# Shift and scale of the first channel mixer: from sums on VectorE to products on TensorE

## The chip, the cores and the metric

The kernel runs on one core of one Trainium2 chip. The metric is device time in microseconds for the whole trunk: two layers at 256 tokens and 2048 channels, everything in 32-bit floats. Three runs of the kernel before gave a median of 2667.47 us (2666.54 to 2671.47).

## The reference, cut to what matters

Each layer turns a conditioning vector `c` into six vectors of 2048 values: a shift, a scale and a gate for the token mixer, and the same three for the channel mixer.

```python
c_act = jax.nn.silu(c)
for i in range(DEPTH):
    mod = c_act @ ada_w[i] + ada_b[i]
    sh_m, sc_m, g_m, sh_f, sc_f, g_f = jnp.split(mod, 6, axis=-1)
    h = modulate(rms_norm(x, norm_mix_g[i]), sh_m, sc_m)
    out = ...                     # layer 0: RWKV-7 time mix, layer 1: conformer convolution
    x = x + g_m[:, None, :] * out
    h = modulate(rms_norm(x, norm_ffn_g[i]), sh_f, sc_f)
    x = x + g_f[:, None, :] * conv_glu_ffn(h, ffn_w_up[i], ffn_w_dw[i], ffn_b_dw[i], ffn_w_down[i])
return rms_norm(x, final_norm_g)
```

`ada_w[i]` is 2048 x 12288, so one of the six pieces is a 2048 x 2048 matrix (16 MB) that meets a single vector. The change is about pieces 3 (`sh_f`) and 4 (`sc_f`) of layer 0.

## The kernel before, in words

Channels lie on the 128 partitions and tokens along the free dimension, so each of the 2048 channels belongs to one of `KT` = 16 tiles of 128 x 256. A dense weight tile is loaded as 128 x 2048 (1 MB) into a buffer named `raw`, of which there are four. It is split into a rounded part `hi` (ScalarE, line 231) and a rest `lo` (VectorE or GpSimd, line 232), and three TensorE products (lines 237 to 239) stand for one exact one.

Layer 0 runs through these stages; the times are those of the profiled execution.

- 0 to 190 us: normalise x, mix tokens, part of the k products. Here `ada_s` makes shift and scale of the token mixer as products (line 367): the vector silu(c) stands as a stationary operand of 128 x 32 (`cc`, one real column), 256 columns of `ada_w` stream past it, and four such products write to the four 32-partition groups of a PSUM tile. ScalarE copies the result out (line 371) and a product with a column of constants (line 373) adds up the four groups and turns the row of 128 values into a column.
- 190 to 412 us: the rest of k, then r and most of v, and the inverse of small triangular matrices.
- 412 to 731 us: the scan, and beside it the rest of v, group norm, gate, and half of the output projection for five tiles.
- from 731 us on: output projection, channel mixer of layer 0 (ConvGLU), layer 1.

The other pieces of the modulation are made by `ada(l, piece, f)` as jobs on VectorE: load 1 MB of the transposed weights into a `raw` buffer, multiply by silu(c) spread over all partitions and sum up in a custom instruction (line 208); for layer 0 in two halves of 1024, each followed by a short read of the accumulator. Jobs stand in the list `jobs`, and `bg(n)` takes the next n. Before the scan, the list starts with pieces 4 and 3 of all 16 tiles (32 jobs); `bg` takes ten of them in the k and r stages. For the scan, five gates (piece 2) are put in front and seven at the end, so that 34 jobs are made during it.

The order of TensorE in the scan is written by hand: each piece of work is a Python generator that yields the planned time until its next step, a heap calls the generators by planned time, and TensorE executes the products in just that order. `PD` = 13 planned units pass from one tile of the scan to the next. The orders of the other engines and of the DMA queue (all of these loads go through SyncE) are left to the tile framework's scheduler, which tracks buffers and inserts the waits. Every queue is executed in its order: an instruction that waits holds up all that stand behind it.

In the scan, `prep_gen` prepares a tile (lines 687, 688, 702, 721, 730, 736), `chain_gen` carries the state through its four chunks (lines 750, 758, 763, 769, 776), `v_gen` and `wo_gen` are dense products, and `gn_gen` is group norm and gate (lines 786, 799, 804). Masked copies out of PSUM (line 156) and the state update (lines 159 and 774) are on VectorE, other copies (lines 689, 694, 755, 765) on ScalarE.

Of the kernel before, what the change touches and what calls it, by code (L numbers as in the profile page):

```python
# [11 lines left out]
F32 = mybir.dt.float32  # L12
F32R = mybir.dt.float32r
AF = mybir.ActivationFunctionType
ALU = mybir.AluOpType
# [3 lines left out]
P = 128  # L19
T = 256  # L20
C = 2048
KT = C // P
# [27 lines left out]
BGT = 10.0  # L50
# [12 lines left out]
BGN = 16  # L63
BGT2 = 7
WACT = 1
TQ = 2
NWO = 5
# [4 lines left out]
NG = 12  # L72
# [8 lines left out]
SLAG = 2  # L81
BX = 2
CME = {mybir.EngineType.PE}
KAPPA = math.exp(-0.5)
# [27 lines left out]
def trunk_kernel(ctx: ExitStack, tc: tile.TileContext, a, out):  # L112
    nc = tc.nc
    cp = ctx.enter_context(tc.tile_pool(name="cp", bufs=1))
# [11 lines left out]
    def slot(dt=F32):  # L126
        if dt == F32R:
            return pool.tile([P, 2, SLOT], F32R, tag="s2", bufs=NS, name=nm("s"))
        return pool.tile([P, 2, SLOT], F32, tag="s2", bufs=NS, name=nm("s"))

    def slot512():
        return slot().rearrange("p a t -> p (a t)")[:, :2 * T]
# [4 lines left out]
    def raw_tile():  # L137
        return pool.tile([P, 2048], F32, tag="raw", bufs=4, name=nm("raw"))
# [24 lines left out]

    # ---- constants, parameters
    cst = cp.tile([P, NCC], F32, name="cst")
# [19 lines left out]
    geff = [cp.tile([P, 2 * KT], F32, name=f"geff{i}") for i in range(2)]  # L185
# [31 lines left out]
    jobs = []  # L217
# [4 lines left out]

    # ---- linear layers
    def split_w(r, k0, k1, step=1024, eng=None):
# [39 lines left out]
    class k_outer:  # L264
        """some outputs together, the operands fed one at a time; the weights split ahead, two operands' at once"""

# [39 lines left out]

    # ---- rms norm
    def sq_acc(st, x):
        s = t1()
        act(s, x, AF.Square)  # L310
        if st[0] is None:
            st[0] = s
        else:
            vadd(st[0], st[0], s)
# [9 lines left out]

    # ================= layer 0: time mix =================
    hs = [slot() for _ in range(KT // 2)]
# [10 lines left out]
    rstd = rstd_of(st)  # L337
# [10 lines left out]
    tg = cp.tile([P, 2, T], F32, name="tg")  # L348
    cc = slot512().rearrange("p (k m) -> p k m", k=KT)
    nc.gpsimd.memset(cc, 0.0)  # L350
# [4 lines left out]
    ahead = {}  # L355

    def ada_s(f):
        lw = slot().rearrange("p a t -> p (a t)")[:, :448]
        nc.sync.dma_start(out=lw, in_=a["lw1"][f])
        # scale and shift of tile f  # L360
        pa = ps("y")
        for q in range(2):
            r = raw_tile()
            nc.sync.dma_start(out=r, in_=a["ada_s"][f, q])
            for k in range(8):
                g, kk = k % 4, 8 * q + k
                nc.tensor.matmul(pa[32 * g:32 * g + 32, :T], lhsT=cc[:, kk, :], rhs=r[:, k * T:(k + 1) * T],  # L367
                                 start=kk < 4, stop=kk >= 12, skip_group_check=True)
        rk = load_w(a["w_k"][f])
        sb = t1()  # L370
        nc.scalar.copy(sb, pa[:, :T])
        for j in range(2):
            nc.tensor.matmul(pa[:, 256 + j:257 + j], lhsT=sb[:, j * P:(j + 1) * P], rhs=K("e4"), start=True, stop=True, skip_group_check=True)
        for j in range(2):
            piece = 1 - j
            vadd(mod(0, piece, f), pa[:, 256 + j:257 + j], pc("ada_b", piece * KT + f))
        stt(geff[0][:, f:f + 1], mod(0, 1, f), 1.0, pc("gam_mix", f), ALU.add, ALU.mult)
        ahead[f] = (lw, rk)

    ada_s(0)  # L380
    for f in range(KT):
# [11 lines left out]
        for k0 in range(0, KM, KM // 2):  # L393
            hi, lo = split_w(rk, k0, k0 + KM // 2)
            for m in range(k0, k0 + KM // 2):
                c = slice((m - k0) * P, (m - k0 + 1) * P)
                d = kps[m // 2][:, (m % 2) * T:(m % 2) * T + T]
# [25 lines left out]

    for f in range(KT):
        jobs += [(0, 4, f), (0, 3, f)]

# [9 lines left out]

    # ---- k, decay, a; A, B, K of the scan; N
    for f in range(KM, KT):
# [126 lines left out]

    # ---- inverse of the 32-blocks, all heads and chunks on partitions
    X = raw_tile()
# [65 lines left out]

    # ---- v, scan, group norm, bonus, gate
    def small(tag, w, bufs):
# [36 lines left out]
    def prep_gen(f):  # L672
        ari, bk, tt, tn = ld.pop(f)
        v = vt.pop(f)
# [5 lines left out]
        yield 0  # L680
        # products of A, R with B, K, and B, K by tokens
        for c in range(NC_):
# [12 lines left out]
            yield PU  # L695
        # off-diagonal block of the inverse
        py = ps("g")
# [5 lines left out]
        for h in range(2):  # L703
            r1 = slice(h * L + 32, h * L + 64)
            nc.scalar.copy(ysb[r1].rearrange("p c t -> p (c t)"), py[r1, :P])
        # bonus
        rk = t1()
# [6 lines left out]
        yield PU  # L714
        # centred V by tokens, in the other half of the partitions
        pvt = ps("g")
# [107 lines left out]

    # half of the output projection and residual, while the scan goes on
    def wo_gen(m):
# [10 lines left out]
    def bg_gen(n):  # L837
        for i in range(n):
            bg(1)
            yield BGT if i < BGN else BGT2  # L840

    heap, seq = [], [0]

    def at(t, g):
        heapq.heappush(heap, (t, seq[0], g))
        seq[0] += 1
# [7 lines left out]
    for fs in ((0, 1, 2, 3), (4, 5, 6, 7), (8, 9, 10, 11), (12, 13), (14, 15)):  # L854
        at((fs[-1] + 3) * PD + 3.0, gn_gen(fs))
    jobs[:0] = [(0, 2, f) for f in range(NWO)]
    jobs += [(0, 2, f) for f in range(NWO, NG)]
    at(0, bg_gen(99))
    for m in range(NWO):
        at(WO0 * PD + m * WOP, wo_gen(m))  # L860
    with tc.manual_schedule(engines={mybir.EngineType.PE}):
        while heap:
            t, _, g = heapq.heappop(heap)
            if isinstance(g, tuple):
                g = chain_gen(g[1], PD / 6)
            d = next(g, None)
            if d is not None:
                at(t + d, g)
    # ---- output projection and residual
    # gain * x, with the shift in the last columns: the products of the two are rstd-free  # L870
    def operand(l, which, f):
# [29 lines left out]

    # ---- ConvGLU
    def ffn(l, st, ops, nops):
# [54 lines left out]

    # ================= layer 1: conformer convolution =================
    ops = nops  # L960
    rstd = rstd_of(st)
# [22 lines left out]

    # n of the taps on the tensor engine, m on GpSimd, the others on the vector engine in two chains
    def tap(f, d):
# [12 lines left out]
    def taps(f, u, us, dg):  # L999
# [13 lines left out]
        rest = list(range(n + m + 1, 31))  # L1013
        x = BX if f < KT - 1 else BXL
        h = (len(rest) + 1) // 2 + x
# [29 lines left out]
    late = None  # L1045
    with tc.manual_schedule(engines=CME):
        for f in range(KT):
# [5 lines left out]
            pa = linear(a["w_pw1"][f], ops, "mm", T + 2, e1, LST)  # L1053
# [9 lines left out]
        with tc.manual_schedule(engines=TME):  # L1063
# [16 lines left out]
            for i in range(4):  # L1080
                d = dg[:, i * P:(i + 1) * P]
# [9 lines left out]
            for f in range(max(KT + 4, AST + NAQ)):  # L1091
# [3 lines left out]
                g = f - 1  # L1095
                if 0 <= g < KT:
                    act(tv[g], tv[g], AF.Silu, bias=pc("cln_b", g), scale=pc("cln_g", g))
                g = f - 2
# [3 lines left out]
                g = f - 3  # L1102
                if 0 <= g < KT:
                    (nc.gpsimd if g % XP == XP - 1 else nc.vector).tensor_tensor(
                        out=cops[g][:, 1, :T], in0=tv[g], in1=cops[g][:, 0, :T], op=ALU.subtract)
# [19 lines left out]

    # ---- final norm
    rstd = rstd_of(st)
# [56 lines left out]
def _layout(i):  # L1184
    i = {k: np.asarray(v) for k, v in i.items()}
    c = np.ascontiguousarray
    d = {}
# [20 lines left out]
    aw = i["ada_w"][0].reshape(2, 8, P, 6, KT, P)[:, :, :, 1::-1]  # L1208
    d["ada_s"] = c(aw.transpose(4, 0, 2, 1, 3, 5)).reshape(KT, 2, P, C)
    d["w_k"] = c(i["rwkv_w_rkv"][0, 1][:, :KM * P]).reshape(KT, P, KM * P)  # L1210
    d["lw1"] = c(np.concatenate([i["rwkv_w1"][0], i["rwkv_a1"][0], i["rwkv_g1"][0]], 1).reshape(KT, P, 448))
# [24 lines left out]
```

## Time and profile before

| | |
|---|---|
| median of three runs | 2667.47 us (2666.54 to 2671.47) |
| span of the profiled execution | 2670.5 us |
| instructions | 52899 |
| mean granted TensorE clock | 0.977 |
| busy: TensorE, VectorE, ScalarE, GpSimd | 94%, 75%, 51%, 17% |

The profiled execution is one of its own; its span lies inside the range of the three runs. "Busy" is the time that an engine's instructions cover. TensorE overlaps the loading of stationary operands (shown as an engine of its own, PEld) with products, and the ends of products are modelled; so a busy TensorE may still have room. The granted clock is the share of full speed that the chip gave TensorE over a stretch; it has two levels, 2.4 GHz (1.0) and 1.2 GHz (0.5).

### The profile page before, as it was taken

The page shows a single profiled execution, that of the slowest core. Times are in us where ns is not written, and L with a number is a line of the kernel's source. Part 1 is how long each engine was busy: PE and PEld are TensorE (multiplying, and loading weights), DVE is VectorE, ACT ScalarE, POOL GpSimd, SP SyncE. Part 2 cuts the span into 40 slices and gives each one's busy share as a digit, 9 for nine tenths or more (in the row PEclk, how much of TensorE's full clock was granted, in tenths as well). Part 3 has the DMA queues.
Part 4 walks back from the last instruction along what each step waited for, and adds up shares of the span by engine and source line. Part 5 has one row for each costly group of instructions (what it writes and reads, how often), then busy time and mean ns, then how long its engine had stood idle before and what let it go on. Part 6 is the DMA issues. An engine that isn't in the chain of part 4 may idle for free.

```text
span 2670.5 us, 52899 instructions
## 1 busy us (share of the span) xinstructions
PE 2520.7 (94%) x21250; PEld 2404.8 (90%) x21250; DVE 2003.9 (75%) x3635; ACT 1357.1 (51%) x2650; POOL 464.0 (17%) x452
## 2 busy tenths in 40 slices
PE   6899996999999999999999999978899999999998
PEld 3678885877799999999999999967899999999997
DVE  4567767768688888887878979979988656656665
ACT  4565622556555543553455555554555445534553
POOL 0000015544000012001100248954200000000000
PEclk9999997989999999999999999989999999999999
DMA  8887766677277778777978844436777655555553
GB/s 312 316 312 268 211 207 209 230 218 240 78 284 278 283 285 331 292 281 290 336 263 296 305 161 164 168 127 243 286 275 273 220 188 188 170 190 190 178 175 126
DMA packets 154805, 630.84 MB, mean 236 GB/s; under 512 B 60480, under 2 KB 72256, under 8 KB 95936
## 3 DMA queue, kind: packets, MB, share of 16 engines
q1 hardware_dynamic: 153824, 624.85, 65.9%
q8 instruction: 166, 2.72, 0.4%
q0 software_dynamic: 736, 2.62, 0.3%
q14 instruction: 79, 0.65, 0.1%
HBM read 614.30 MB, written 13.11 MB: 235 GB/s over the span
## 4 chain that ended last, share of the span: by engine, by line
PE 76%; DVE 10%; DMA 7%; ACT 3%; issue 2%; POOL 1%; SPq 0%; DVEq 0%; POOLq 0%; ACTq 0%
PE ps L237 22%; PE ps L239 22%; PE ps L238 21%; DMA raw<-ada 4%; DVE raw L208 3%; DVE s L159 2%; DVE lo L232 1%; PE ps L367 1%; PE ps L300 1%; DMA raw<-ada_s 1%; POOL lo L232 1%; DVE s L156 1%; PE ps L687 1%; ACT hi L231 1%; PE ps L398 1%
## 5 line engine op out<-in xcount | busy, mean ns | idle before, releaser
L237 PE MATMUL ps<-s,hi 128*128 128x258 f32 (+1 forms) x5584 | 1594.8, 286 | 7.5 <-ACT hi L231 6.4
L239 PE MATMUL ps<-s,lo 128*128 128x258 f32 (+1 forms) x5584 | 1581.6, 284 | 20.8 <-DVE lo L232 18.9
L238 PE MATMUL ps<-s,hi 128*128 128x258 f32 (+1 forms) x5584 | 1579.8, 283 | 0.6 <-DVE s L153 0.6
L231 ACT CAST hi<-raw 128x1024 fp32r<-128x1024 f32 (+6 forms) x873 | 769.7, 897 | 881.8 <-PE ps L238 606.1
L239 PEld LDWEIGHTS ps<-s,lo 128*128 128x128 f32 x5584 | 1063.7, 191 | 29.4 <-DVE lo L232 22.8
L237 PEld LDWEIGHTS ps<-s,hi 128*128 128x128 f32 x5584 | 1060.2, 190 | 16.8 <-ACT hi L231 8.6
L238 PEld LDWEIGHTS ps<-s,hi 128*128 128x128 f32 x5584 | 1063.4, 190 | 4.5 <-issue 3.0
L232 DVE TENSOR_TENSOR lo<-raw,hi 128x1024 fp32r<-128x1024 f32 (+4 forms) x639 | 746.0, 1171 | 303.5 <-ACT hi L231 301.8
L232 POOL TENSOR_TENSOR lo<-raw,hi 128x512 fp32r<-128x512 f32 x234 | 335.2, 1458 | 957.5 <-ACT hi L231 623.4
L208 DVE CUSTOM_DVE_ANT_0 raw<-raw,cb,par 128x1024 f32<-128x1024 f32 x156 | 213.2, 1367 | 76.0 <-DMA raw<-ada 71.3
L208 DVE CUSTOM_DVE_ANT_0 raw<-raw,cb,md 128x1024 f32<-128x1024 f32 x156 | 214.9, 1378 | 0.9
L159 DVE SCALAR_TENSOR_TENSOR s<-ps,par,s 128x239 f32<-128x239 f32 (+26 forms) x420 | 166.0, 456 | 1.8 <-ACT s L162 1.2
L1135 POOL TENSOR_TENSOR s<-s,t 128x256 f32<-128x256 f32 x6 | 4.1, 727 | 751.4 <-DVE t L322 751.4
L156 DVE TENSOR_TENSOR t<-ps,t 128x256 f32<-128x256 f32 x188 | 79.2, 422 | 47.5 <-PE ps L239 43.8
L159 DVE SCALAR_TENSOR_TENSOR s<-ps,md,s 128x256 f32<-128x256 f32 x117 | 55.9, 480 | 41.8 <-PE ps L239 41.7
L159 DVE SCALAR_TENSOR_TENSOR t<-t,par,t 128x255 f32<-128x255 f32 (+1 forms) x172 | 82.6, 480 | 1.9 <-ACT t L162 0.6
L156 DVE TENSOR_TENSOR s<-ps,cst 64x64 f32<-64x64 f32 (+2 forms) x208 | 48.1, 253 | 37.7 <-ACT n L689 27.0
L162 ACT ACTIVATE t<-t,par 128x256 f32<-128x256 f32 x118 | 68.1, 587 | 5.6 <-DVE t L156 2.5
L162 ACT ACTIVATE t<-t 128x256 f32<-128x256 f32 x102 | 42.5, 417 | 37.9 <-DVE t L159 24.1
L687 PE MATMUL ps<-s,s 128*128 128x128 f32 x256 | 46.6, 308 | 11.6 <-ACT s L694 10.6
L300 PE MATMUL ps<-s,raw 128*128 128x256 f32 x256 | 56.0, 380 | 0.0
L300 PEld LDWEIGHTS ps<-s,raw 128*128 128x128 f32 x256 | 48.4, 190 | 6.9 <-issue 0.3
(199 smaller groups left out, 2167.2 us busy)
## 6 DMA issues: line engine op xcount, KB each, us to landing
raw<-w_up SPq DMA_DIRECT2D x172, 1024.0 KB, 4.9
raw<-ada SPq DMA_DIRECT2D x156, 1024.0 KB, 6.7
raw<-w_dn SPq DMA_DIRECT2D x64, 896.0 KB, 4.7
raw<-w_pw SPq DMA_DIRECT2D x48, 1024.0 KB, 4.9
raw<-w_rkv SPq DMA_DIRECT2D x38, 1024.0 KB, 6.0
raw<-ada_s SPq DMA_DIRECT2D x32, 1024.0 KB, 6.4
raw<-w_dn SPq DMA_DIRECT2D x32, 960.0 KB, 4.9
raw<-w_o SPq DMA_DIRECT2D x11, 1024.0 KB, 4.9
```

The costliest lines, as they stand in the source:

```text
L156: nc.vector.tensor_tensor(out=o, in0=x, in1=y, op=ALU.mult)
L159: nc.vector.scalar_tensor_tensor(out=o, in0=x, scalar=s, in1=y, op0=op0, op1=op1)
L162: nc.scalar.activation(out=o, in_=i, func=func, bias=bias, scale=scale)
L208: nc.vector.tensor_tensor_reduce(out=r[q], in0=r[q], in1=cb[:, q * w:(q + 1) * w], scale=1.0, scalar=mod(l, piece, f) if q else pc("ada_b" ...
L231: nc.scalar.copy(hi[:, s], v[:, s])
L232: (eng or nc.vector).tensor_tensor(out=lo[:, s], in0=v[:, s], in1=hi[:, s], op=ALU.subtract)
L237: nc.tensor.matmul(acc[:, :n], lhsT=hi[:, c], rhs=x[:, 0, :n], start=first, stop=False)
L238: nc.tensor.matmul(acc[:, :n], lhsT=hi[:, c], rhs=x[:, 1, :n], start=False, stop=False)
L239: nc.tensor.matmul(acc[:, :n], lhsT=lo[:, c], rhs=x[:, 0, :n], start=False, stop=last)
L300: nc.tensor.matmul(acc[:, :T], lhsT=r[:, k * P:(k + 1) * P], rhs=hs32[k], start=k == 0, stop=k == n - 1)
L367: nc.tensor.matmul(pa[32 * g:32 * g + 32, :T], lhsT=cc[:, kk, :], rhs=r[:, k * T:(k + 1) * T], start=kk < 4, stop=kk >= 12, skip_group_che ...
L687: nc.tensor.matmul(pg[:, h * P:(h + 1) * P], lhsT=bkc, rhs=ari[h][:, c].rearrange("p j t -> p (j t)"), start=True, stop=True, skip_group_c ...
```

## The change

Pieces 3 and 4 of layer 0 leave the job list. A new generator, `ada_gen`, makes them during the scan in the way of `ada_s`: for each of the 16 tiles two loads of 1 MB, two groups of eight products of 128 x 32 by 256 columns (each product is two instructions in the trace), a ScalarE copy, two products that sum up and turn, and three tiny VectorE operations. It is planned to load at once, multiply `AGL` = 5 units later, sum up `AGC` = 1.5 units after that, and start the next tile 14.5 units after this one. Its PSUM tile has the tag `g`, of which there are three buffers, shared with `prep_gen` and `gn_gen`. The job list now holds the twelve gates first: ten of them are made where pieces 4 and 3 were made before, two in the scan. `cc` gets a buffer of its own, so that it lives until the scan. The weights get a second layout, `ada_f`, made on the host with the others. Removed comment lines are left out here.

```diff
@@ -80,6 +80,9 @@
+AGL = 5.0
+AGC = 1.5
+AGT = 14.5
@@ -346,7 +349,7 @@
-    cc = slot512().rearrange("p (k m) -> p k m", k=KT)
+    cc = cp.tile([P, KT, 32], F32, name="cc")
@@ -421,8 +424,7 @@
-    for f in range(KT):
-        jobs += [(0, 4, f), (0, 3, f)]
+    jobs += [(0, 2, f) for f in range(NG)]
@@ -837,7 +839,33 @@
         for i in range(n):
             bg(1)
-            yield BGT if i < BGN else BGT2
+            yield BGT
+
+    def ada_gen():
+        for f in range(KT):
+            rs = []
+            for q in range(2):
+                rs.append(raw_tile())
+                nc.sync.dma_start(out=rs[q], in_=a["ada_f"][f, q])
+            yield AGL
+            pa = ps("g")
+            for q in range(2):
+                for k in range(8):
+                    g, kk = k % 4, 8 * q + k
+                    nc.tensor.matmul(pa[32 * g:32 * g + 32, :T], lhsT=cc[:, kk, :], rhs=rs[q][:, k * T:(k + 1) * T],
+                                     start=kk < 4, stop=kk >= 12, skip_group_check=True)
+                if q == 0:
+                    yield 0.5
+            sb = t1()
+            nc.scalar.copy(sb, pa[:, :T])
+            yield AGC
+            for j in range(2):
+                nc.tensor.matmul(pa[:, 256 + j:257 + j], lhsT=sb[:, j * P:(j + 1) * P], rhs=K("e4"), start=True, stop=True, skip_group_check=True)
+            for j, piece in enumerate((4, 3)):
+                vadd(mod(0, piece, f), pa[:, 256 + j:257 + j], pc("ada_b", piece * KT + f))
+            stt(geff[0][:, KT + f:KT + f + 1], mod(0, 4, f), 1.0, pc("gam_ffn", f), ALU.add, ALU.mult)
+            yield AGT - AGL - AGC - 0.5
@@ -853,9 +881,8 @@
-    jobs[:0] = [(0, 2, f) for f in range(NWO)]
-    jobs += [(0, 2, f) for f in range(NWO, NG)]
     at(0, bg_gen(99))
+    at(0, ada_gen())
@@ -1207,6 +1234,8 @@
+    aw = i["ada_w"][0].reshape(2, 8, P, 6, KT, P)[:, :, :, 4:2:-1]
+    d["ada_f"] = c(aw.transpose(4, 0, 2, 1, 3, 5)).reshape(KT, 2, P, C)
```

## Rows read from the trace of the kernel before

**Rows 1.** Page, part 4: share of the span by engine on the last chain.

```profile
PE 76%; DVE 10%; DMA 7%; ACT 3%; issue 2%; POOL 1%; SPq 0%; DVEq 0%; POOLq 0%; ACTq 0%
```

**Rows 2.** Scan by stretches: length, busy PE, PEld, DVE, ACT, POOL, clock, DMA share, GB/s.

```profile
475.00:505.00 30.00, 29.41 (x363) 26.15 (x363) 21.67 (x58) 18.92 (x69) 19.00 (x16) 1.00 0.62 188
575.00:600.00 25.00, 20.55 (x238) 18.16 (x236) 17.16 (x52) 12.69 (x52) 4.37 (x6) 0.73 0.78 235
431.00:455.00 24.00, 15.29 (x123) 14.06 (x123) 7.59 (x20) 8.82 (x27) 9.83 (x8) 0.67 0.64 202
455.00:700.00 245.00, 226.20 (x2551) 191.92 (x2550) 184.64 (x476) 146.42 (x511) 106.73 (x108) 0.94 0.68 222
```

**Rows 3.** VectorE groups, 412 to 731 us: busy, mean ns, idle before.

```profile
L208 DVE CUSTOM_DVE_ANT_0 raw<-raw,cb,md 128x1024 f32<-128x1024 f32 x34 | 50.0, 1470 | 0.5
L208 DVE CUSTOM_DVE_ANT_0 raw<-raw,cb,par 128x1024 f32<-128x1024 f32 x34 | 49.5, 1455 | 14.5 <-DMA raw<-ada 10.7 <-DMA tn<-dTn 2.5 <-POOL s L753 0.7
```

**Rows 4.** Chain of waits, 455 to 700 us: its shares by line.

```profile
by line: DMA raw<-ada 13.6%; DVE raw L208 12.2%; PE ps L687 7.8%; PE ps L237 4.8%; issue 4.6%; PE ps L799 4.3%; POOL lo L232 3.9%; PE ps L750 3.9%; PE ps L238 3.3%; DVE s L156 3.3%; PE ps L239 3.2%; PE ps L688 3.0%; PE ps L763 2.8%; PE ps L
```

**Rows 5.** What TensorE waited for, 455 to 700 us: total us, times, longest.

```profile
PE ps L750 <- DVE s L159: 5.4, 6, 1.8
PE ps L702 <- ACT s L694: 3.0, 1, 3.0
PE ps L750 <- DVE s L774: 2.6, 3, 1.3
```

**Rows 6.** Timeline of one wait in the scan: start, duration, instruction, idle before.

```profile
579.79 1.29 DVE L208 CUSTOM_DVE_ANT_0 raw<-raw,cb,par 128x1024 f32<-128x1024 f32 x1 [2.69 <-DMA raw<-ada]
...
581.80 0.27 ACT L694 COPY s<-ps 128x128 f32<-128x128 f32 x1 [2.80 <-DVE s L156]
...
582.12 0.44 PE L702 MATMUL ps<-tn,n 32*32 32x32 f32 x16 [2.99 <-ACT s L694]
```

**Rows 7.** Timeline of TensorE around one half of `ada_s`, clock 1.0.

```profile
92.69 1.07 PE L367 MATMUL ps<-raw,s 128*32 128x256 f32 x16
93.69 0.39 PE L399 MATMUL ps<-s,hi 128*128 128x256 f32 x1
93.91 0.28 PE L400 MATMUL ps<-s,lo 128*128 128x256 f32 x1
...
96.74 0.50 PE L373 MATMUL ps<-cst,t 128*128 128x1 f32 x4
```

**Rows 8.** The weight loads of the same products.

```profile
92.69 0.59 PEld L367 LDWEIGHTS ps<-raw,s 128*32 128x32 f32 x16 [0.33 <-issue]
...
96.62 0.53 PEld L373 LDWEIGHTS ps<-cst,t 128*128 128x128 f32 x4
```

**Rows 9.** Timeline of TensorE in the scan: dense products between small ones.

```profile
567.27 0.39 PE L237 MATMUL ps<-s,hi 128*128 128x256 f32 x1
567.50 0.28 PE L238 MATMUL ps<-s,hi 128*128 128x256 f32 x1
...
567.74 0.28 PE L237 MATMUL ps<-s,hi 128*128 128x256 f32 x1
567.86 0.28 PE L238 MATMUL ps<-s,hi 128*128 128x256 f32 x1
567.97 0.28 PE L239 MATMUL ps<-s,lo 128*128 128x256 f32 x1
568.18 0.44 PE L702 MATMUL ps<-tn,n 32*32 32x32 f32 x16
```

**Rows 10.** Waits of TensorE, 40 to 190 us, on the inputs of `ada_s`.

```profile
PE ps L373 <- ACT t L371: 4.4, 9, 0.5
PE ps L367 <- DMA raw<-ada_s: 4.2, 2, 2.7
```

**Rows 11.** Waits of the DMA queue in the scan, 412 to 731 us.

```profile
SPq L205 <- POOL lo L232: 44.3, 7, 13.4
```

**Rows 12.** DMA issues in the scan: number, size, median us to landing.

```profile
raw<-ada SPq DMA_DIRECT2D x33, 1024.0 KB, 5.4
```

## The prediction, made before the changed kernel was run

> **What bounds the kernel now.** I read the chain that ended last, then the scan by stretches, then what stands on that chain inside the scan, and at last the spacing of single products. Over the whole span TensorE holds 76% of the chain [rows 1]; the reader is to see that time taken from another engine counts only where TensorE stands still for it. The removed work lies in the scan, and the scan looks different: from 455 to 700 us the transfers of the removed jobs hold 13.6% of the chain and their sums on VectorE 12.2%, together 25.8% of 245 us, or 63 us [rows 4]. That is tempting. But a chain tells only what came last at each step, not how far the next thing was behind. So I look at TensorE itself: in these 245 us it is covered for 226.2 us, that is, it visibly stands idle for 18.8 us, and its granted clock is 0.94 on the mean [rows 2]. With levels of 1.0 and 0.5 this is 12% of the time, 29 us, at the lower one, which costs at most half of that, 14.7 us. These two numbers, 33.5 us, are about all that VectorE can give back here.
>
> The idle time does come from VectorE: products of the state update wait for lines 159 and 774 (5.4 and 2.6 us), line 702 for a copy on ScalarE (3.0 us) [rows 5], and that copy in turn had waited 2.8 us for VectorE, where a job had stood 2.69 us waiting for its load and then summed for 1.29 us [rows 6]. A queue is executed in order, so the small masked copies behind the job waited too. The lower clock goes with such gaps: 0.73 in 575 to 600 us, where TensorE is covered 20.55 of 25 us, against 1.00 in 475 to 505 us, where it is covered 29.41 of 30 [rows 2].
>
> **What the change takes away.** In the scan 34 jobs are summed, 68 instructions of 50.0 + 49.5 = 99.5 us [rows 3]. Two stay, so 32 x 2.93 = 94 us leave VectorE in the scan. VectorE is covered 184.6 of 245 us [rows 2], so it is no bound itself; what counts is TensorE's waiting. Ten gates take the places of ten jobs before the scan: the same instructions on the same 1 MB loads, less one tiny operation for a scale; nothing. Loads in the scan: 34 of 1 MB before, 2 + 32 after, all on the same queue into the same four buffers; the bytes are equal, only their places change.
>
> **What it adds to TensorE.** The first stage of this kernel shows the very same work. At full clock, half a tile (16 instructions of line 367) starts at 92.69 and the next product at 93.69: 1.00 us. The dense product that follows it takes until 93.91, 0.22 us, before the next one starts [rows 7]; between like products in the scan that distance is 0.12 us (567.74 to 567.86), and it is 0.23 us where a small product stood ahead (567.27 to 567.50) [rows 9]. So leaving the block costs another 0.10. Entering one from dense work costs 0.10 more too: the last dense product before line 702 takes 0.21 us (567.97 to 568.18) where 0.11 is usual (567.86 to 567.97) [rows 9]. One half is 1.20 us, two are 2.4. The summing products (line 373, four instructions) take 0.50 us [rows 7]. That gives 2.9 us a tile, and 16 x 2.9 = 46 us. Without any switching it would be 16 x 2.5 = 40; I take 46, because the scan alternates shapes all the time, and keep 40 as the lower end. At the lower clock it would be more, but the clock should rise.
>
> The Trainium skill has the switch as a rule, in "TensorEngine Tiling (Array Packing)", Key Properties: a change of tiling mode drains TensorE first. The spacings above agree (0.21 against 0.11 us), though they hold for changes of the number format as well. By that rule in full the sum is 46, without it 40; it speaks against chopping the work into 32 halves among the dense products.
>
> **What of it is covered.** The first tile is planned for the head of the scan, where TensorE is covered for 15.3 of 24 us at a clock of 0.67 [rows 2]: it is hidden, -3. Of the 18.8 idle us I give back 13: the VectorE part of [rows 5] is 11.0 as shown, some shorter waits add to it, and what is late next (ScalarE's copies) is only a little earlier. Of the 14.7 us lost to the lower clock I give back 10, since the denser the products, the fewer the gaps that it goes with. Some waiting is hidden inside "busy", because the ends of products are modelled: 0 to 10 us, I take 5. The ends are: nothing of all this (TensorE merely gets 46 us more), or all of it, 3 + 18.8 + 14.7 + 10 = 46.5.
>
> **New waits.** TensorE's own queue now holds instructions that wait for loads and for a ScalarE copy, and everything planned behind them waits as well, the state update first. In the first stage line 373 waited 4.4 us in 9 waits for the copy, and line 367 4.2 us in 2 for its load [rows 10]. In the scan the copy has 1.5 planned units and the load 5. The scan runs some 245 units in about 300 us (431 to 731), so that is 1.8 and 6.1 us, against a copy of some tenths and a median landing of 5.4 us [rows 12]. I take +3 for both, from 0 up to the rival below. The PSUM buffer held meanwhile is one of three that `prep_gen` needs; VectorE, which empties them, is freer now, so 0, with up to +5. ScalarE gets 16 copies, VectorE 48 operations on one column: next to the 94 us taken away, nothing, and `cc` moves without an instruction.
>
> **The sum.** 46 + 3 - 3 - 13 - 10 - 5 = +18 us, against 2670.5 us for the profiled execution, so 2688.5 of that kind; the median of the runs lies 3.0 us lower, so 2667.5 + 18 = 2685.5. VectorE is relieved of work on which TensorE waits only in part, and TensorE gets the work in full.
>
> **Rivals.**
> - *The chain through VectorE really sets the pace* (faster). Then the 63 us of [rows 4] go and the 46 take their place: -17, 2650.5. For it: the chain. Against it: in 475 to 505 us TensorE is covered 29.41 of 30 us at full clock [rows 2] although jobs are summed there too. It decides if more than 46 us of waiting can be got back, that is, if over 12 us are hidden inside "busy" on top of every visible one.
> - *The work fits into TensorE's room* (no change). Counted by weight loads, TensorE is occupied for 191.9 of 245 us [rows 2] and has 53 us of room; the new loads take 0.59 + 0.59 + 0.53 a tile [rows 8], 27 us in all. They would fit, and with the waits of VectorE gone the order by hand just runs on: 2667.5. Against it: small products and switches are limited by other things than loads. The Trainium skill, "Perfetto Trace Analysis", Identifying the Most-Contended Engine, holds that room on TensorE is to be judged by weight-load occupancy and not by covered time; by that rule this rival would be the forecast.
> - *TensorE waits for loads as VectorE did* (slower still). Issue of the jobs' loads was itself held up 44.3 us, in 7 waits, for GpSimd to let go of a buffer [rows 11], and transfers stand for 13.6% of 245 = 33 us on the chain [rows 4]. If a buffer comes free later than about 0.7 us after its planned place (6.1 - 5.4), each such load stands in TensorE's queue: 18 + up to 33, some 2710. Against it: a pair of buffers is back 6 units after its load, 8 before the next.
> - *The change does less than it says* has no room: no product of pieces 3 and 4 is left on VectorE, and none can be left out.
>
> **Chances.** Forecast 0.55, faster rival 0.16, the fitting one 0.14, the waiting one 0.15. The range takes in the bounds of the sum (40 - 46.5 is -6.5, or 2661) and part of both outer rivals: 2656 to 2712. The runs of before lie within 0.2% of each other, and 0.2%, 5.3 us, is about what a measurement of this kernel can tell from no change. Slower by more than that: 0.55 less 0.05 for a forecast that comes out small, plus 0.15, is 0.65. Within: 0.14 + 0.05 = 0.19. Faster: 0.16.
>
> **What would show it.** Right: TensorE in the scan is covered for 96% or more with a clock near 1.00, the scan ends some 18 us later (at about 749), line 367 takes about 1.0 us a half, and VectorE falls by some 94 us there; all later stages take as long as before. The fitting rival would show a scan of the same length with the same cover. Wrong in its size: TensorE waits with `raw<-ada_f` or the copy in front of it. Wrong altogether: the scan ends before 731 us, which means that waiting was hidden inside covered time.

## The result, and the profile of the changed kernel

The changed kernel took 2692.9 us, the median of four runs (2682.8 to 2694.3), beside 2667.0 us for the kernel before (2663.5 to 2671.5). The ratio is 1.0087 with an interval of 1.0068 to 1.0106, so it is slower, by 23 us of 2667 (18 to 28). The forecast was 2685.5 us, +18. The profiled execution spans 2690.6 us and lies at the median of its runs; that of before lies some 5 us above the median of its own (a run's time has 2 us on top of the span of the same execution, 2692.65 against 2690.6 here). This is to be kept in mind where single executions are compared.

The chain that ended last has moved to TensorE, as its line in the profile of after shows (compare [rows 1]: 76% there):

```profile
PE 80%; DVE 9%; DMA 6%; ACT 2%; issue 2%; SPq 1%; POOL 1%; DVEq 0%; ACTq 0%; POOLq 0%
```

To compare the scans I cut each at the start of the same instructions: the first product of line 687 (689 after), which opens the preparation of a tile, the first of line 763 (765), the last of line 687 (689), and the last of line 804 (806). That gives a head, a middle and a tail. First before, then after; the columns are those of [rows 2], and the last row of each is the whole scan.

```profile
413.10:452.90 39.80, 20.55 (x157) 18.88 (x157) 24.86 (x62) 9.45 (x28) 21.49 (x18) 0.70 0.56 173
452.90:694.10 241.20, 222.59 (x2466) 189.13 (x2465) 180.64 (x463) 143.56 (x499) 106.73 (x108) 0.94 0.70 229
694.10:722.90 28.80, 24.60 (x258) 17.74 (x257) 14.44 (x37) 15.09 (x55) 0.00 (x0) 1.00 0.04 11
413.10:722.90 309.80, 267.74 (x2877) 225.75 (x2876) 219.95 (x560) 168.10 (x581) 128.22 (x126) 0.91 0.62 201
```

```profile
416.60:458.60 42.00, 22.92 (x193) 20.07 (x192) 19.02 (x56) 8.79 (x27) 16.03 (x16) 0.72 0.67 216
458.60:707.80 249.20, 242.69 (x2926) 196.45 (x2925) 94.11 (x362) 145.88 (x508) 87.43 (x110) 0.99 0.59 194
707.80:749.50 41.70, 36.15 (x339) 25.19 (x337) 19.23 (x49) 19.28 (x64) 0.00 (x0) 0.80 0.35 121
416.60:749.50 332.90, 301.77 (x3453) 241.70 (x3451) 132.35 (x465) 173.95 (x598) 103.47 (x126) 0.93 0.57 188
```

The reader is to see four things. The scan is 23.1 us longer, as much as the loss by the ratio; the two profiled executions differ by 20.1 us, since that of after comes to the scan 3.5 us later and takes 6.5 us less behind it. The middle does what was forecast: TensorE is covered for 242.7 of 249.2 us (97.4%) at a clock of 0.99, where it had 222.6 of 241.2 at 0.94, and VectorE falls from 180.6 to 94.1 us. But the middle carries only 8 of the 23 us; the tail is 13 us longer, at a clock of 0.80 where it had 1.00. And VectorE loses 87.6 us over the scan, which is longer all the same.

What is left of the sums in the scan, and the new products, in the groups by line from 416 to 750 us (compare [rows 3] and [rows 7]; lines 208 and 367 of before are 211 and 370 now, the new products are line 856, the summing ones line 864):

```profile
L211 DVE CUSTOM_DVE_ANT_0 raw<-raw,cb,par 128x1024 f32<-128x1024 f32 x2 | 2.6, 1285 | 7.0 <-DMA raw<-ada 7.0
...
L856 PE MATMUL ps<-raw,cc 128*32 128x256 f32 x512 | 33.6, 384 | 1.4 <-DMA raw<-ada_f 1.4
L864 PE MATMUL ps<-cst,t 128*128 128x1 f32 x64 | 9.2, 247 | 1.0 <-ACT t L861 0.8
```

TensorE waited 1.4 us for the new loads and 1.0 before the summing products, in the whole scan. Its other waits, 416 to 750 us, in the form of [rows 5]:

```profile
PE ps L732 <- DMA s<-dT: 7.8, 1, 7.8
PE ps L689 <- ACT s L696: 6.3, 3, 5.9
...
PE ps L240 <- ACT hi L234: 2.7, 1, 2.7
PE ps L752 <- DVE s L162: 1.4, 2, 0.8
PE ps L856 <- DMA raw<-ada_f: 1.4, 1, 1.4
...
PE ps L752 <- DVE s L776: 0.4, 1, 0.4
```

The waits for VectorE that stood in [rows 5], 8.0 us, are down to 1.8, both of line 752. What is late instead is in the chain of the middle (458.6 to 707.8 us, shares by line, to be held against [rows 4]):

```profile
by line: PE ps L689 9.5%; PE ps L856 9.2%; PE ps L240 8.0%; PE ps L801 5.4%; PE ps L241 5.3%; PE ps L242 5.3%; DMA raw<-w_o 4.7%; DMA raw<-w_rkv 4.7%; PE ps L752 4.4%; PE ps L765 4.4%; PE ps L723 3.9%; PE ps L690 3.8%; PE ps L771 3.4%; PE p
```

The 25.8% of jobs are gone. In their place stand TensorE's own lines and two loads that have nothing to do with the change, those of the dense products' weights, `w_o` and `w_rkv`: together 9.4% of 249 us, 23 us.

### The profile page after: what moved, and what is told of

It reads as the page before. It is cut to its first block, busy times and chain, and to the rows that moved or that the text cites. A ratio compares the mean times of both kernels' runs of the same rounds, so it can differ in the third digit from the quotient of the medians.

```text
span 2690.6 us, 54020 instructions
## 1 busy us (share of the span) xinstructions
PE 2555.3 (95%) x21826; PEld 2423.0 (90%) x21826; DVE 1919.0 (71%) x3539; ACT 1361.2 (51%) x2666; POOL 443.3 (16%) x452
## 4 chain that ended last, share of the span: by engine, by line
PE 80%; DVE 9%; DMA 6%; ACT 2%; issue 2%; SPq 1%; POOL 1%; DVEq 0%; ACTq 0%; POOLq 0%
PE ps L240 23%; PE ps L241 22%; PE ps L242 22%; DVE raw L211 2%; DVE s L162 2%; DVE lo L235 1%; PE ps L370 1%; DMA raw<-ada 1%; PE ps L856 1%; PE ps L689 1%; DMA raw<-ada_s 1%; DVE s L159 1%; PE ps L801 1%; ACT hi L234 1%; DMA raw<-w_o 1%
## 5 line engine op out<-in xcount | busy, mean ns | idle before, releaser
L242 PEld LDWEIGHTS ps<-s,lo 128*128 128x128 f32 x5584 | 1064.3, 191 | 22.9 <-DVE lo L235 18.5
L235 POOL TENSOR_TENSOR lo<-raw,hi 128x512 fp32r<-128x512 f32 x234 | 327.3, 1425 | 962.5 <-ACT hi L234 758.9
L211 DVE CUSTOM_DVE_ANT_0 raw<-raw,cb,par 128x1024 f32<-128x1024 f32 x124 | 168.1, 1356 | 47.5 <-DMA raw<-ada 47.2
L211 DVE CUSTOM_DVE_ANT_0 raw<-raw,cb,md 128x1024 f32<-128x1024 f32 x124 | 168.0, 1355 | 0.4
L370 PE MATMUL ps<-raw,cc 128*32 128x256 f32 x512 | 40.1, 433 | 12.5 <-DMA raw<-ada_s 4.3
```

Of the source, the lines that this page charges most:

```text
L211: nc.vector.tensor_tensor_reduce(out=r[q], in0=r[q], in1=cb[:, q * w:(q + 1) * w], scale=1.0, scalar=mod(l, piece, f) if q else pc("ada_b" ...
L235: (eng or nc.vector).tensor_tensor(out=lo[:, s], in0=v[:, s], in1=hi[:, s], op=ALU.subtract)
L242: nc.tensor.matmul(acc[:, :n], lhsT=lo[:, c], rhs=x[:, 0, :n], start=False, stop=last)
```

## The experiments

Two theories. **Full price**: the products take their full time on a nearly full TensorE, and VectorE gives back only the visible waits and the low clock. Its rivals: the products fit in, and the loss comes from the loads or from their places; or the loss is an accident of the order by hand. The first four kernels take the change apart. Each ratio is to runs of the kernel before on the same chip, and is given in us at 2667.

### Neither sums nor products

`e1_no_ada` leaves pieces 3 and 4 out altogether:

```diff
+    nc.vector.memset(md[0][:, 3 * KT:5 * KT], 0.0)
+    nc.vector.memset(geff[0][:, KT:2 * KT], 1.0)
...
-    at(0, ada_gen())
```

> Leaves out pieces 3 and 4 of layer 0 altogether (shift 0, scale times gain 1): neither the sums on VectorE nor the loads, products and copies of ada_gen; the rest is the changed kernel. It shows what VectorE's relief gives back by itself, against the kernel before, and what ada_gen costs, against the kernel after. Theory (products in full on a nearly full TensorE): 46 us of products cost 46, and 20 to 25 of them come back, so about 2640 to 2647. Rival (room on TensorE is ample, loads and buffers are what costs): the relief would be small, 2655 to 2667. If it came out under 2635, the relief is larger than the idle time and the lower clock together, and something in ada_gen costs more than its products.

Measured: 0.9905 (0.9878 to 0.9932), 25 us less than before (18 to 33). That is all that taking 94 us of sums off VectorE is worth. The middle and then the whole scan:

```profile
452.00:663.00 211.00, 207.97 (x2466) 177.72 (x2465) 92.11 (x328) 142.56 (x499) 84.72 (x108) 1.00 0.34 98
413.90:692.10 278.20, 255.26 (x2876) 215.56 (x2875) 125.62 (x412) 167.09 (x581) 103.37 (x126) 0.96 0.35 103
```

The same 2466 product records as before in the middle now take 211.0 us instead of 241.2. Idle time there falls from 18.6 to 3.0 us, 15.6 less. The clock goes from 0.94 to 1.00; 6% of 241.2 is 14.5. The two add up to 30.1 of the 30.2 us that are gone. As far as a clock given to 0.01 can tell (0.01 is 2.4 us here), no more waiting was hidden inside covered time in this middle. The two profiled scans differ by 31.6 us, more than the 25 by the medians, so these sizes hold for two single executions.

### The products without their loads

`e2_no_loads` is the changed kernel with its products reading a tile that is there anyway, so its pieces 3 and 4 come from other numbers:

```diff
-                rs.append(raw_tile())
-                nc.sync.dma_start(out=rs[q], in_=a["ada_f"][f, q])
+                rs.append(cb)
```

> The changed kernel, but the products of ada_gen read the resident tile of silu(c) and not freshly loaded weights: the 32 loads and their buffers are gone, every product, copy and sum stays; pieces 3 and 4 are therefore not the reference's. Theory (the products themselves cost): as the kernel after or a few us less, 2683 to 2693. Rival (the loads' buffers cost: the loads of the output projection come late at the end of the scan, and what used to fill the waits there is missing): 2655 to 2678, with the end of the scan (last preparation product to last group norm product) back from 42 to about 30 us.

Measured: 1.0041 (1.0020 to 1.0063), +11 us. The median of 2676.7 us falls into the range of the rival, not of the theory: the loads do cost something. Middle, tail, whole scan:

```profile
448.60:692.60 244.00, 240.72 (x2935) 194.94 (x2934) 97.12 (x367) 148.50 (x511) 84.71 (x108) 1.00 0.30 87
692.60:728.80 36.20, 32.55 (x329) 22.05 (x328) 15.80 (x44) 16.29 (x59) 0.00 (x0) 0.87 0.03 8
410.30:728.80 318.50, 295.26 (x3452) 235.77 (x3452) 131.10 (x460) 174.51 (x598) 102.36 (x126) 0.96 0.30 91
```

Against `e1_no_ada` the products cost 1.0041 - 0.9905 = 0.0136, 36 us (27 to 46), and 40.3 us in the two scans. The middle holds 469 more product records, 13 tiles at 36 records, and is 33.0 us longer: 2.54 us a tile at full clock. So the products are paid in full, even where TensorE hardly waits for loads or for VectorE. Of the 40.3 us, idle time makes 0.3 (23.2 against 22.9). The tail is 36.2 us, so 7.4 of the 12.9 us that the tail of after has over that of before are there without the new loads: two of the tiles (72 product records) stand in it.

The rival that the work fits into the room counted by weight loads falls here. In the middle of `e1_no_ada` weight loads occupy TensorE for 177.7 of 211.0 us, so 33 us of room; what was put in brings 194.9 - 177.7 = 17 us of weight loads. It would have fitted twice, and it cost 33. The Trainium skill, "Perfetto Trace Analysis", Identifying the Most-Contended Engine, wants TensorE's room judged by weight-load occupancy, beside its arithmetic against the peak; here the measurement differs, for products on 32 of the 128 columns among full ones.

### The loads without their products

`e3_loads_only` keeps the 32 loads, and of each tile only one product of 32 columns per load, which reads the buffer and so lets go of it; pieces 3 and 4 aren't computed:

```diff
-                for k in range(8):
-                    ...
+                nc.tensor.matmul(pa[:32, 32 * q:32 * q + 32], lhsT=cc[:, q, :], rhs=rs[q][:, :32],
+                                 start=True, stop=True, skip_group_check=True)
```

> The changed kernel with all 32 loads of ada_gen at their places and each buffer held as long, but of the eight products of a load only one of 32 columns is left, and no copy and no sums follow: pieces 3 and 4 are left out (shift 0, scale times gain 1). The counterpart of the run without loads. Theory: close to the kernel without any of the work, 2642 to 2652. Rival (loads and buffers cost): 2668 to 2690, with the long end of the scan still there.

Measured: 0.9954 (0.9934 to 0.9973), 12 us less than before, so 13 us (4 to 22) more than `e1_no_ada`. The median of 2653.5 us lies just above the theory's range and far below the rival's. From the other side, after less `e2_no_loads`, the loads cost 1.0087 - 1.0041 = 0.0046, 12 us (5 to 20). Both agree. The scan of `e3_loads_only` shows it in its middle (this execution lies 7 us above the median of its runs):

```profile
461.80:685.80 224.00, 215.97 (x2509) 182.97 (x2509) 88.76 (x325) 141.09 (x498) 86.91 (x110) 0.98 0.66 218
```

8 us are idle there against 3.0 in `e1_no_ada`, and the clock is 0.98 against 1.00. The three parts are then 25 us less for the sums, 36 more for the products and 12 more for the loads, +23. Taken like this they close by themselves, since each is a difference of neighbouring kernels; what tests the division is the second value for the loads, 13 against 12.

### Tiles closer together

`e4_agt12` plans a tile every 12 units instead of 14.5, so that all are done before the tail:

```diff
-AGT = 14.5
+AGT = 12.0
```

> The changed kernel with one number changed: a tile of ada_gen every 12 planned units and not every 14.5, so that the last one falls at 185 and not at 222 and the buffers are free when the output projection's loads are wanted. Theory (products in full wherever they stand): 2688 to 2695, the end of the scan shorter, the middle longer by as much. Rival (late buffers at the end of the scan cost some 10 us): 2678 to 2684.

Measured: 1.0064 (1.0044 to 1.0084), +17 us; against after that is 6 us less, but the two intervals overlap, so it isn't told apart. The median of 2684.4 us lies between the ranges of the theory and the rival. Middle and tail:

```profile
460.00:716.10 256.10, 247.29 (x3006) 199.12 (x3005) 97.54 (x372) 151.07 (x518) 88.56 (x112) 0.99 0.60 205
716.10:745.20 29.10, 25.86 (x257) 18.23 (x257) 14.35 (x37) 15.01 (x55) 0.00 (x0) 0.94 0.04 10
```

The tail is 29.1 us again, where before had 28.8. The head and the middle have grown by what it gave up: the scan is 332.5 us (412.7 to 745.2), that of after 332.9. What was gone in one place had to be paid in the other.

### The dense products' loads earlier

The chain of after named `w_o` and `w_rkv`. `e7_dense_lead` is the changed kernel with these loads issued 6 units ahead of their products in the scan:

```diff
+LEAD = 6.0
...
     def v_gen(f):
+        r = load_w(a["w_rkv"][2, f])
+        yield LEAD
         acc = ps("mm")
-        r = load_w(a["w_rkv"][2, f])
-        yield 0
...
-        at((V1 + i * VP) * PD, v_gen(f))
+        at((V1 + i * VP) * PD - LEAD, v_gen(f))
```

(and the same for `wo_gen`)

> The changed kernel with one change: the loads of the dense tiles in the scan (v and output projection) are placed 6 planned units ahead of their products, ahead of the loads of ada_gen that stand between, so that the buffers go to them first. The runs without loads and with loads alone put some 12 to 14 us on the loads of ada_gen. If these come from dense tiles that get their buffer late: 2678 to 2686. If they come from anything else that the loads do (traffic, the DMA queue's issue, TensorE waiting for ada_f itself): 2688 to 2696, or slower if ada_f is now late.

Measured: 1.0049 (1.0029 to 1.0068), +13 us, so 10 us (3 to 17) of the 23 came back. The chain of its middle, 460.3 to 710.2 us:

```profile
by line: PE ps L690 11.4%; PE ps L241 10.6%; PE ps L857 9.6%; PE ps L242 6.7%; PE ps L243 6.7%; PE ps L753 4.8%; PE ps L766 4.8%; PE ps L691 4.6%; DMA raw<-w_o 4.4%; PE ps L802 4.2%; PE ps L772 3.9%; PE ps L724 3.5%; PE ps L779 3.0%; PE ps 
```

`w_rkv` has left the head of this list, `w_o` has stayed. The scan of its profiled execution is 329.0 us, only 4 shorter than that of after; that execution lies 7 us above the median of its runs, so it does not show where the rest was won. Whether the same lead would also gain something without the new loads was not tried.

### Four blocks in place of two

The forecast had put 0.2 us on every entering and leaving of a block. `e11_four_blocks` is `e2_no_loads` with each group of eight products cut in two, planned as 32 blocks more:

```diff
+                    if k == 3:
+                        yield 0.5
-            yield AGT - AGL - AGC - 0.5
+            yield AGT - AGL - AGC - 1.5
```

> The run of the changed kernel's products without loads, with the sixteen products of a tile in four blocks of four, half a planned unit apart, and not in two of eight: 32 more insertions among other work, not one product more. Pieces 3 and 4 are not the reference's, since the products read the resident tile. If each insertion costs the two switches of the prediction, 0.10 to 0.20 us: 3 to 7 us slower than the run without loads, 2680 to 2684 where that one gave 2676.7. If an insertion costs nothing (neighbours in the scan switch shapes anyway): within 2 us of it, 2675 to 2679.

Measured: 1.0030 (1.0010 to 1.0050) against 1.0041 of `e2_no_loads`: 3 us less, with bounds of 11 less and 5 more. Counted in the trace, the new products stand in 49 separate blocks where `e2_no_loads` has 29, so 20 more and not 32: often no other work was planned between two parts. 20 x 0.2 = 4 us lies inside the bounds, so these times can't tell. The middle and one of its blocks can:

```profile
447.90:693.90 246.00, 244.11 (x2934) 193.47 (x2933) 98.15 (x366) 148.99 (x512) 84.82 (x108) 1.00 0.30 89
```

```profile
454.24 0.64 PE L855 MATMUL ps<-cb,cc 128*32 128x256 f32 x8
454.81 0.34 PE L752 MATMUL ps<-s,s 128*64 128x64 f32 x4
```

With 41 blocks where `e2_no_loads` has 24, as many products and the same full clock, it is 2.0 us longer (246.0 against 244.0) and covered 3.4 us longer (244.1 against 240.7): 0.12 to 0.20 us for each of the 17. Most of that stands in the blocks themselves. Eight instructions take 0.57 us until the next product starts (454.24 to 454.81) and sixteen 1.00 (713.61 to 714.61 of after, shown below), so a block that is cut in two costs 0.14 us. For what its neighbours lose, which is what the forecast put at 0.2, an estimate from these rows leaves 0.06 us at most. The Trainium skill, "TensorEngine Tiling (Array Packing)", Key Properties, has a drain at each change of tiling mode; these traces fit it with 0.12 to 0.20 us a block, but do not show that it is a drain.

### What is it in the sums that costs?

Three kernels undo parts of the kernel before, without the change. `e5_load_ahead` issues each job's load one job earlier, so that VectorE need not wait for it:

```diff
...
+        held = []
         for i in range(n):
-            bg(1)
+            if jobs:
+                job, r = jobs.pop(0), raw_tile()
+                nc.sync.dma_start(out=r, in_=a["ada"][job])
+                held.append((job, r))
+            if held and (i >= 1):
+                job, r = held.pop(0)
+                ada(*job, r)
```

> The kernel before, all of it, with one change: in the scan a job's load is issued one job (7 to 10 planned units) ahead of its sums, so that it has landed when VectorE comes to them. The run without any of the work gave back 25 us against the kernel before. Theory A (VectorE's queue is held up by jobs that stand waiting for their loads): 10 to 20 us come back, 2647 to 2657. Theory B (it is held by the sums themselves, 1.28 us each, and the load's waiting is hidden): within 4 us of before, 2663 to 2671. Rival C (a second buffer of the four is now held by jobs, and the dense tiles' loads come late): 2670 to 2685.

Measured: 0.9981 (0.9963 to 0.9999), 5 us less (0 to 10). `e9_quarters` cuts a job into four sums where it had two, and `e10_ahead_quarters` does both:

```diff
-TQ = 2
+TQ = 4
```

> The kernel before, all of it, with the jobs of layer 0 that were summed in two halves of 1024 now summed in four quarters of 512, so that a masked copy or a state update waits behind at most a quarter. Theory (the sums hold VectorE's queue, the time per sum counts): a few us faster, 2655 to 2665. Rival (the total of VectorE's time counts, and four accumulator reads and fixed costs a job make it longer): 2668 to 2680.

> The kernel with the jobs' loads one job ahead in the scan (5 us faster than before by its ratio) and, besides, sums in quarters. If the two gains are of different kinds (a queue held by loads, a queue held by sums), they add up: 2650 to 2660. If quarters only lengthen the jobs: 2666 to 2678.

Measured: 0.9998 (0.9984 to 1.0013) and 1.0005 (0.9990 to 1.0021). Neither differs from before, and the small gain of the earlier loads isn't there in the second, so I don't build on it. Then `e8_sums_no_loads`, in which the scan's jobs of pieces 3 and 4 sum a tile that is there anyway and load nothing:

```diff
-            nc.sync.dma_start(out=r, in_=a["ada"][l, piece, f])
+            if not NOLOAD[0]:
+                nc.sync.dma_start(out=r, in_=a["ada"][l, piece, f])
...
-                out=r[q], in0=r[q], in1=...
+                out=r[q], in0=cb[:, q * w:(q + 1) * w] if NOLOAD[0] else r[q], in1=...
```

> The kernel before, but the 22 jobs for pieces 3 and 4 that fall into the scan sum the resident tile of silu(c) with itself and load nothing; the sums, their buffers and everything else stay, and pieces 3 and 4 are therefore not the reference's for those tiles. Together with the run without any of the work (25 us faster than before) it splits VectorE's part into the sums and the loads. Theory A (waiting for loads): 2645 to 2656. Theory B (the sums themselves): 2660 to 2668.

Measured: 1.0061 (1.0039 to 1.0083), 16 us **slower**, with 22 MB less to load. No theory of mine had that. Its middle, and its waits from 412 to 745 us (lines 753 and 777 are 750 and 774 of before, line 159 is the same):

```profile
455.60:714.60 259.00, 231.32 (x2467) 196.76 (x2466) 182.59 (x463) 144.37 (x499) 105.02 (x108) 0.89 0.40 124
```

```profile
PE ps L753 <- DVE s L159: 11.2, 6, 3.4
PE ps L753 <- DVE s L777: 9.3, 4, 4.2
```

TensorE waits 20.5 us for VectorE here where [rows 5] have 8.0 (8.8 over the whole scan of before), the longest time 4.2 us where it was 1.8, and the clock of the middle is 0.89. (This execution lies 11 us above the median of its runs, so the sizes are rough.) A job is two sums. Where sums follow each other on VectorE without small work between them, in runs of two or three, the middle has ten such runs, and four in before. A load ahead of a sum spaces the sums out; without it they stand in rows ahead of the small copies that the state update waits for. That reading fits the rows, but no run changed the spacing by itself.

No kernel here that computes what the reference does beats the kernel before by more than these measurements can tell.

## Why the prediction came out right, and where a term was off

The direction held, and the time lay inside the range, 7 us above the forecast (5 by the ratio). By its own steps:

- **What bounds the kernel.** Right, and this decided it. The chain gave 63 us to the jobs, TensorE's visible idle time and clock 33.5. Leaving the sums out (`e1_no_ada`) gave 25 us by the medians and 31.6 by the profiled scans. The faster rival, by which the chain's share would go, is refuted.
- **The relief, 13 + 10 + 5 = 28.** Right in the sum: 25 (18 to 33). In the middle of the profiled scan its terms were 15.6 us of idle time, 14.5 of clock and nothing that shows as hidden inside covered time. The 5 us for hidden waits made up for two other terms taken a little low.
- **The products, 46 - 3 = 43.** Too much by some 7 by the medians, 36, though their interval (27 to 46) still holds 43; 40 in the scans. The middles are the sharper measure, both at full clock with 3 us idle: 2.54 us a tile, where the forecast had 2.9. The step that failed is the 0.10 us for entering and 0.10 for leaving a block. The single spacings it was read from ([rows 7, 9]) are there, but they do not add up over the blocks: 2.54 is 0.04 a tile above the products and sums alone (2.5), and `e11_four_blocks` leaves the neighbours 0.06 us a block at most. That they switch shapes without the block too would explain it, and was not tried. The lower end, 16 x 2.5 = 40, less 3 for the hidden tile, was the right value. The first tile hidden in the head held: heads of 38.1 us (`e1_no_ada`) and 38.3 (`e2_no_loads`). One half took 1.00 us in the scan too (713.61 to 714.61 below), as [rows 7] had it.
- **New waits, +3.** As written, TensorE's waits for its own load and for the copy, they were right: 1.4 and 0.8 us. But the loads cost 12 (5 to 20), and this is the term that was mis-sized: 3 for all new waits. The step that failed stands under "What the change takes away": that only the places of the loads change, and so nothing is due. Two loads of a tile hold two of the four buffers until TensorE has read them, and other loads on the queue wait behind. From the row of [rows 11] I had looked only at what this would do to the new products, not to the dense ones. The queue of after, 416 to 750 us, where line 850 issues the new loads and line 247 the dense weights:

```profile
SPq L850 <- POOL lo L235: 38.1, 7, 12.5
...
SPq L247 <- PE ps L752: 11.5, 2, 10.3
...
SPq L247 <- PE ps L856: 6.6, 3, 5.3
```

The tail shows one such case. In the timeline of after, a load of `w_o` goes out at 714.74, just when the new products have read a buffer; its data lets ScalarE begin at 719.99, and TensorE has stood still for 2.73 us:

```profile
713.61 1.07 PE L856 MATMUL ps<-raw,cc 128*32 128x256 f32 x16
714.61 0.34 PE L752 MATMUL ps<-s,s 128*64 128x64 f32 x4
...
714.74 7.90 SPq L247 DMA_DIRECT2D raw<-w_o  x3
...
719.99 1.04 ACT L234 CAST hi<-raw 128x1024 fp32r<-128x1024 f32 x1 [2.82 <-DMA raw<-w_o]
...
721.08 0.58 PE L240 MATMUL ps<-s,hi 128*128 128x256 f32 x1 [2.73 <-ACT hi L234]
```

Set over the whole scans, the 14.4 us between `e2_no_loads` and after are 7.9 us more of idle time (31.1 against 23.2) and a clock of 0.93 against 0.96 (3% of the 302 us covered: 9; the clock is given to 0.01, so this is 9 give or take 3). In the tail it fell to 0.80, that is, part of it ran at 1.2 GHz. The two profiled executions differ by 12.9 us as a whole: 6.3 before the scan, these 14.4 in it, and 7.8 less behind it. That the loads of the dense products come late is supported by `e7_dense_lead`, which got 10 (3 to 17) of the 12 us back by them; that it is the pairs that hold them up was argued from the queue and not tried.

- **The sum.** 28 against 25, 43 against 36, 3 against 12: +18 against +23. Two errors of opposite sign, 7 too much and 9 too little, and 3 too much of relief; each measured term is known to 7 to 9 us. That the forecast came so near is luck in part.
- **The rivals.** "It fits into TensorE's room": refuted by `e2_no_loads`. "TensorE waits for loads as VectorE did": its mechanism was there mainly in another place, at 12 us and not 33: TensorE waited 1.4 us behind the new loads, and the dense ones came late.
- **What would show it.** Cover of 97.4% and a clock of 0.99 hold for the middle; over the whole scan they are 90.6% and 0.93, as the forecast did not foresee the tail. The scan ended at 749.5 us (forecast about 749), but it also began 3.5 us later. Whether that comes from the change isn't shown: the scan begins between 409.4 and 416.3 us in the kernels without the new loads, and between 412.7 and 420.2 in those with them. VectorE lost 87.6 us, not 94: 48 tiny operations took 8.2 where I had written next to nothing, some 7 us of small ones went with the sums, and instructions that follow each other overlap in the trace (by 13 us in before, 5 in after), which covered time counts once.
- **Later stages as before.** They were not: from the end of the scan to the end they took 1941.1 us, before 1947.6. The four profiled kernels with the new loads in the scan took 1938.7 to 1941.6 there, the eight without them 1944 to 1949. So about 6 us behind the scan go with these loads, which hides a part of what they cost in it; why is not shown.

Open is why one job of sums costs the scan about 0.8 us (25 / 32) at all, when neither its load's wait nor the length of its instructions makes that up alone; `e8_sums_no_loads` points to their spacing.

## What to carry to other kernels

Cost work that is moved off an engine by the idle time and the lost clock of the engine that it held up (33 us here, 25 came), not by its share of the chain (63) or its busy time (94); cost the same work on the full engine by what it takes until the next product starts, 16 x 2.5 us, whatever room its weight loads seem to leave. Where a moved load takes two buffers in place of one, look for the other loads behind it on its queue: the moved work waited only 1.4 us for its own loads here, and the loads still cost 12. And take such a change apart, all of it out, its loads out, its products out: three kernels gave all three terms, and two errors that nearly cancelled became visible.

## What the runs showed of the hardware

Fewer loads made the kernel slower: 22 MB less, 16 us more (`e8_sums_no_loads`). That waiting for a load had spaced VectorE's work out is my reading, which no run tried by itself. And GpSimd's speed went with VectorE's sums: the same 42 subtractions of the scan took 1.77 us each before and 1.50 after, when VectorE was covered 88 us less. In the five kernels with the sums in the scan they took 1.72 to 1.77 us, in the seven without 1.47 to 1.55. The loads do not decide it: 1.75 with the sums but not their loads (`e8_sums_no_loads`), 1.54 with the new loads but no sums (`e3_loads_only`). The first row is of before (413 to 723 us), the second of after (417 to 750 us):

```profile
L232 POOL TENSOR_TENSOR lo<-raw,hi 128x512 fp32r<-128x512 f32 x42 | 73.7, 1773 | 86.5 <-ACT hi L231 72.0 <-PE ps L238 10.0 <-ACT n L689 4.4
```

```profile
L235 POOL TENSOR_TENSOR lo<-raw,hi 128x512 fp32r<-128x512 f32 x42 | 61.6, 1497 | 84.5 <-ACT hi L234 84.4
```
